# Stick-breaking attention in a hybrid block: the causal mask moved from a matrix product into the scan, and three copies of q moved from VectorE to ScalarE

## The chip, the core and the metric

The kernel runs on one core of a Trainium2 chip. The core has five engines with instruction queues of their own, each worked off in order: TensorE (PE, matrix products and transposes, into PSUM), VectorE (DVE), ScalarE (ACT, functions of one operand, copies and casts), GpSimd (POOL) and SyncE (SP, which here only issues DMAs). Engines wait for each other by semaphores. PE's weight loads have a row of their own in the profile, PEld. The metric is the time of one execution on the device in microseconds (us); several executions are timed, and one more is taken with the hardware profiler.

## The reference

One layer of a decoder trunk, for 1024 positions of width 1024 in float32. The part that matters is one of three head groups: attention of 8 heads of width 64 without a softmax. Keys take shares of a stick, the nearest first.

```python
def stick_breaking_attention(q, k, v):
    ...
        z = jnp.einsum('bqhd,bkhd->bhqk', qi, kj) * scale
        ...
        causal = s_pos < t_pos
        log_beta = jax.nn.log_sigmoid(z)
        log_rem = jnp.where(causal, jax.nn.log_sigmoid(-z), 0.0)
        suffix = lax.cumsum(log_rem, axis=3, reverse=True) - log_rem
        weights = jnp.where(causal, jnp.exp(log_beta + suffix), 0.0)
        o = jnp.einsum('bhqk,bkhd->bqhd', weights, vj)
```

q and k are RMS-normalised per head before that. A key that is not strictly before its query leaves the rest of the stick whole (factor 1) and gets weight 0.

## The kernel before

All matrix products are made of float32 halves: an operand is split into a high part, rounded to the type that PE multiplies (`split`: ScalarE makes the high part, VectorE or GpSimd the rest), and a product is three matmuls (`product`, L165 to L167), or two where one operand is used rounded.

The stages: the norm of the input and the gating group's projection; then for four pairs of heads the projection of q, k and v (`project`, PSUM tiles `qkv_ps`, two banks that it shares with the convolution's `cv_ps`) and the attention (`attend`); the convolution group; the output projection; the two large feed-forward products (`f_ps`, `d_ps`) and the gate (`g_ps`).

While the attention of pair n runs, the projection of pair n+1 (with the last pair, the convolution's projection) is woven between its pieces: `weave` draws from two generators in proportion to a count of matmuls. This order is the program's; a scheduler of the framework then sets each engine's order from a timeline of its own, so that a small change can move many instructions by some places.

`project` works on 8 tiles of 128 positions. Each tile fills a `qkv_ps` bank with 24 matmuls. ScalarE squares q and k (`qk_sq`), VectorE sums (`ss`), GpSimd takes the power (`rs`), VectorE scales (`qk`), and v is split into `V` (ScalarE, then VectorE, L141 and L142), which frees the bank. After every second tile `turn_qk` transposes q and k (`qk_tr`, in one of three PSUM banks that it shares with the attention's `w_tr`), and writes the high part of q (`QS`), its rest (`low_q`), the high part of k (`KH`) and its rest (`KL`, VectorE, which is the last reader of the `qk_tr` bank). The two heads of a pair lie in the lower and the upper 64 partitions. When a half of the positions is complete, joins build operands with 128 partitions: for k three copies on ScalarE (L411 to L413), for q three copies on VectorE (L414 to L416), each 64 x 512. There are 8 such sets, two for each pair.

`attend` has two pieces for each head and each pair of query blocks. `stick` computes for a query block t the product z over (t + 1) x 128 keys: one matmul with `KH` (L447), one with `KL` (L449), both with `QS` as weights, and for the 512 keys that hold the diagonal a third (L453), the identity times `below`, a constant tile that is -2^60 above the diagonal. ScalarE takes the Sigmoid of -z/8 (L454) into `rem`: the factor that a key leaves, 1 for a masked key. VectorE scans `rem` from the last key to the first, multiplying (L458), and the difference of neighbours (L464, on VectorE for t = 3, 5, 7 and otherwise on GpSimd) gives the weights `wt`. There are three buffers of `rem` and two PSUM banks for z. `gather` transposes the weights (`w_tr`, L486), splits them (`wT_hi`, `wT_lo`, L138 and L139) and multiplies them by `V` (`av`, L504).

Of the kernel before, what the change touches and what calls it, by code (L numbers as in the profile page):

```python
# [6 lines left out]

F32 = mybir.dt.float32
F32R = mybir.dt.float32r
AF = mybir.ActivationFunctionType  # L10
ALU = mybir.AluOpType
AX = mybir.AxisListType

P = 128
T = 1024
# [17 lines left out]
def hybrid_block(ctx: ExitStack, tc: tile.TileContext, a: dict):  # L33
# [5 lines left out]
    nc = tc.nc  # L39
    PSUM = bass.MemoryType.PSUM  # L40

    const = ctx.enter_context(tc.tile_pool(name="const", bufs=1))
# [61 lines left out]
    for _ in range(WARM):  # L104
        nc.tensor.matmul(warm[:, :P], ones, ones, start=True, stop=True)
    ident_r = const.tile([P, P], F32R, name="ident")
# [1 line left out]
    nc.gpsimd.memset(ident, 0.0)  # L108
    nc.gpsimd.affine_select(out=ident_r, in_=ident, pattern=[[-1, P]], base=0,
                            channel_multiplier=1, compare_op=ALU.not_equal, fill=1.0)  # L110

    below = const.tile([P, P], F32R, name="below")
    nc.gpsimd.memset(below.bitcast(F32), 0.0)
    nc.gpsimd.affine_select(out=below, in_=below.bitcast(F32), pattern=[[-1, P]], base=0,
                            channel_multiplier=1, compare_op=ALU.is_gt, fill=-2.0 ** 60)
    mhalf = const.tile([P, 8], F32, name="mhalf")
    nc.gpsimd.memset(mhalf, -0.5)

# [115 lines left out]
    attn_scope = ExitStack()  # L234
    at = attn_scope.enter_context(tc.tile_pool(name="at", bufs=2))
    lo_p, hi_p = slice(0, HD), slice(HD, P)

# [153 lines left out]
    def turn_qk(head, t, qk):  # L393

        QS, KH, KL, _, low_q = head
        th = t // 4
        tr = bank(ps_tr, "qk_tr")
        for i in range(2):
            for j in range(2):
                o = j * 256 + i * P  # L400
                nc.tensor.transpose(tr[:, o:o + P], qk[:, i, j * P:(j + 1) * P], ident)
        ws = slice((t % 4 - 1) * P, (t % 4 + 1) * P)

        split(tr[:, :256], QS[0][th][:, ws], low_q[th][:, ws], scale=gq)
        nc.scalar.activation(KH[0][th][:, ws], tr[:, 256:], AF.Copy, scale=gk)
        for hh, own in enumerate((lo_p, hi_p)):
            nc.vector.scalar_tensor_tensor(out=KL[hh][th][own, ws], in0=tr[own, 256:],
                                           scalar=gk[own], in1=KH[0][th][own, ws],
                                           op0=ALU.mult, op1=ALU.subtract)
        if t % 4 == 3:  # L410
            nc.scalar.copy(KH[1][th][hi_p], KH[0][th][hi_p])  # L411
            nc.scalar.copy(KH[1][th][lo_p], KH[0][th][hi_p])
            nc.scalar.copy(KH[0][th][hi_p], KH[0][th][lo_p])  # L413
            nc.vector.tensor_copy(QS[1][th][hi_p], QS[0][th][hi_p])  # L414
            nc.vector.tensor_copy(QS[1][th][lo_p], low_q[th][hi_p])
            nc.vector.tensor_copy(QS[0][th][hi_p], low_q[th][lo_p])  # L416
        return 8

    PROJECT = KT * 72 + 32
# [1 line left out]
    def attend(pr):  # L421
# [13 lines left out]
        def stick(hh, g):  # L435
            weights[hh, g] = []
            for t in (2 * g, 2 * g + 1):
                W = (t + 1) * P
                th, ts = block(t)

                rem = at.tile([P, T], F32, tag="rem", name=name("rem"), bufs=3)
                wt = at.tile([P, T], F32, tag="wt", name=name("wt"), bufs=4)
                for kh in reversed(range(th + 1)):
# [3 lines left out]
                    nc.tensor.matmul(z, QS[hh][th][:, ts], KH[hh][kh][:, :n],  # L447
                                     start=True, stop=False)
                    nc.tensor.matmul(z, QS[hh][th][:, ts], KL[hh][kh][:, :n],  # L449
                                     start=False, stop=kh < th)  # L450
                    if kh == th:

                        nc.tensor.matmul(z[:, n - P:], ident_r, below, start=False, stop=True)  # L453
                    last_act[0] = nc.scalar.activation(rem[:, ks], z, AF.Sigmoid,  # L454
                                                       scale=-HD ** -0.5)

                back = rem[:, :W][:, ::-1]
                nc.vector.tensor_tensor_scan(out=back, data0=back, data1=back, initial=1.0,  # L458
                                             op0=ALU.mult, op1=ALU.bypass)


                on_vector = t in (3, 5, 7)
# [882 lines left out]
```

## Time and profile before

| what | before |
|---|---|
| median of 3 runs | 1213.11 us (1210.53 to 1213.97) |
| the profiled execution's own time | 1212.77 us |
| its span, from its first to its last instruction | 1211.1 us |
| mean granted clock of TensorE | 0.995 |
| scans L458: number, busy time, median of one | 64, 90.6 us, 1.476 us |
| Sigmoids L454: number, busy time, mean of one | 96, 46.4 us, 0.500 us |

In the lists of groups a row gives the line in the kernel, the engine, the operation, the tile written and the tiles read (without buffer numbers), the partitions and elements, and how many there are; behind the bar come the busy time, the mean duration of one in ns, and the engine's idle time just before them with what ended it. A timeline row gives the start, the duration (of all that the row joins), and the same names. Durations of matmuls overlap, since they are pipelined.

### The profile page before, as it was taken

The page shows a single profiled execution, that of the slowest core. Times are in us where ns is not written, and L with a number is a line of the kernel's source. Part 1 is how long each engine was busy: PE and PEld are TensorE (multiplying, and loading weights), DVE is VectorE, ACT ScalarE, POOL GpSimd, SP SyncE. Part 2 cuts the span into 40 slices and gives each one's busy share as a digit, 9 for nine tenths or more (in the row PEclk, how much of TensorE's full clock was granted, in tenths as well). Part 3 has the DMA queues.
Part 4 walks back from the last instruction along what each step waited for, and adds up shares of the span by engine and source line. Part 5 has one row for each costly group of instructions (what it writes and reads, how often), then busy time and mean ns, then how long its engine had stood idle before and what let it go on. Part 6 is the DMA issues. An engine that isn't in the chain of part 4 may idle for free.

```text
span 1211.1 us, 17645 instructions
## 1 busy us (share of the span) xinstructions
PE 1188.3 (98%) x5852; PEld 1015.5 (84%) x5852; DVE 885.2 (73%) x1310; ACT 595.8 (49%) x1148; POOL 405.0 (33%) x472
## 2 busy tenths in 40 slices
PE   9999999999999999999999999999999999999997
PEld 7899899899878888888888888888888888888886
DVE  7846788989887667877877777787665656753597
ACT  7735555565643356734333343355443444546542
POOL 2324435465453312034453544421023301013412
PEclk9999999999999999999999999999999999999999
DMA  9602349989654776779998999677889975644857
GB/s 317 225 18 106 112 152 277 251 176 186 144 117 100 179 265 207 214 189 267 264 251 241 251 244 263 213 258 271 307 261 307 284 260 172 221 155 114 177 162 208
DMA packets 127964, 254.04 MB, mean 210 GB/s; under 512 B 14496, under 2 KB 22432, under 8 KB 127168
## 3 DMA queue, kind: packets, MB, share of 16 engines
q1 hardware_dynamic: 94992, 168.08, 41.5%
q0 software_dynamic: 27664, 57.05, 25.2%
q10 hardware_dynamic: 5216, 27.79, 6.3%
q8 instruction: 46, 0.75, 0.3%
q14 instruction: 46, 0.38, 0.1%
HBM read 192.30 MB, written 92.80 MB: 235 GB/s over the span
## 4 chain that ended last, share of the span: by engine, by line
PE 85%; DVE 7%; DMA 4%; issue 2%; ACT 1%; POOL 0%; ACTq 0%; SPq 0%; DVEq 0%; POOLq 0%
PE f_ps L814 25%; PE d_ps L814 25%; PE g_ps L814 6%; PE qkv_ps L165 3%; PE qkv_ps L166 3%; PE qkv_ps L167 3%; DVE rem L458 2%; PE av L504 2%; PE w_tr L486 2%; PE vu_ps L167 1%; PE vu_ps L165 1%; PE vu_ps L166 1%; PE o_ps L167 1%; PE o_ps L165 1%; PE o_ps L166 1%
## 5 line engine op out<-in xcount | busy, mean ns | idle before, releaser
L139 DVE TENSOR_TENSOR w_lo<-raw,w_hi 128x512 fp32r<-128x512 f32 x280 | 240.8, 864 | 87.4 <-ACT w_hi L138 85.5
L138 ACT CAST w_hi<-raw 128x512 fp32r<-128x512 f32 x280 | 172.0, 619 | 241.1 <-PE d_ps L814 121.0
L814 PE MATMUL f_ps<-hn_hi,w_hi 128*128 128x512 f32 x448 | 175.1, 392 | 0.0
L814 PE MATMUL f_ps<-hn_hi,w_lo 128*128 128x512 f32 x448 | 174.9, 391 | 0.0
L814 PE MATMUL f_ps<-hn_lo,w_hi 128*128 128x512 f32 x448 | 174.8, 390 | 0.0
L814 PE MATMUL d_ps<-f_hi,w_hi 128*128 128x512 f32 x448 | 174.8, 390 | 0.0
L814 PE MATMUL d_ps<-f_hi,w_lo 128*128 128x512 f32 x448 | 174.3, 389 | 0.0
L814 PE MATMUL d_ps<-f_lo,w_hi 128*128 128x512 f32 x448 | 174.3, 389 | 0.0
L458 DVE TENSOR_TENSOR_SCAN rem<-rem 128x128 f32<-128x128 f32 (+3 forms) x64 | 90.6, 1426 | 19.3 <-ACT rem L454 19.2
L814 PEld LDWEIGHTS f_ps<-hn_hi,w_hi 128*128 128x128 f32 x448 | 84.5, 189 | 17.8 <-issue 0.2
L814 PEld LDWEIGHTS f_ps<-hn_lo,w_hi 128*128 128x128 f32 x448 | 84.5, 189 | 17.7 <-issue 0.2
L814 PEld LDWEIGHTS f_ps<-hn_hi,w_lo 128*128 128x128 f32 x448 | 84.4, 188 | 17.8
L814 PEld LDWEIGHTS d_ps<-f_lo,w_hi 128*128 128x128 f32 x448 | 84.1, 188 | 17.8 <-issue 0.2
L814 PEld LDWEIGHTS d_ps<-f_hi,w_hi 128*128 128x128 f32 x448 | 84.1, 188 | 17.6 <-issue 0.2
L814 PEld LDWEIGHTS d_ps<-f_hi,w_lo 128*128 128x128 f32 x448 | 84.1, 188 | 17.5
L165 PE MATMUL qkv_ps<-whi,xn_hi 128*128 128x384 f32 x256 | 89.7, 350 | 1.1 <-DVE V L142 1.1
L167 PE MATMUL qkv_ps<-whi,xn_lo 128*128 128x384 f32 x256 | 87.6, 342 | 0.0
L166 PE MATMUL qkv_ps<-wlo,xn_hi 128*128 128x384 f32 x256 | 87.4, 341 | 0.0
L139 DVE TENSOR_TENSOR f_lo<-raw,f_hi 128x512 fp32r<-128x512 f32 x112 | 77.1, 718 | 9.6 <-ACT f_hi L138 9.3
L800 POOL TENSOR_TENSOR S<-S,sq 128x512 f32<-128x512 f32 x19 | 27.4, 1441 | 157.8 <-ACT sq L876 157.8
L138 ACT CAST f_hi<-raw 128x512 fp32r<-128x512 f32 x112 | 67.0, 620 | 23.3 <-DMA raw<-f_dram 20.0
L454 ACT ACTIVATE rem<-z 128x128 f32<-128x128 f32 (+3 forms) x96 | 46.4, 500 | 33.0 <-PE z L453 19.2
(252 smaller groups left out, 2656.2 us busy)
## 6 DMA issues: line engine op xcount, KB each, us to landing
raw<-in_w_ff SPq DMA_DIRECT2D x148, 256.0 KB, 4.0
raw<-f_dram SPq DMA_DIRECT2D x112, 256.0 KB, 4.9
raw<-w_sums SPq DMA_DIRECT2D x64, 256.0 KB, 4.1
f_dram<-f SPq DMA_DIRECT2D x48, 256.0 KB, 4.1
f_dram<-t SPq DMA_DIRECT2D x48, 256.0 KB, 3.8
w_sums<-in_w_ff POOLq DMA_DIRECT2D x8, 1024.0 KB, 12.5
w_sums<-w_sums POOLq DMA_DIRECT2D x8, 1024.0 KB, 13.1
raw<-in_w_out SPq DMA_DIRECT2D x28, 256.0 KB, 3.3
```

The source lines that it names most:

```text
L138: last_hi[0] = nc.scalar.copy(hi, src)
L139: low.tensor_tensor(out=lo, in0=src, in1=hi, op=ALU.subtract)
L165: nc.tensor.matmul(ps, lh, rh, start=first and i == 0, stop=False)
L166: nc.tensor.matmul(ps, lh, rl, start=False, stop=False)
L167: done = nc.tensor.matmul(ps, ll, rh, start=False, stop=last and i == len(terms) - 1)
L454: last_act[0] = nc.scalar.activation(rem[:, ks], z, AF.Sigmoid, scale=-HD ** -0.5)
L458: nc.vector.tensor_tensor_scan(out=back, data0=back, data1=back, initial=1.0, op0=ALU.mult, op1=ALU.bypass)
L486: nc.tensor.transpose(tr[:, n:n + P], wts[i][:, kb * P:(kb + 1) * P], ident)
L504: nc.tensor.matmul(av[:, first * P:], lhs, part[:, o:o + m], start=kb == 0 and part is hi, stop=kb == 2 * g + 1 and part is lo)
L800: return eng.tensor_tensor(out=out, in0=x, in1=y, op=ALU.add)
L814: done = nc.tensor.matmul(bank, l, r, start=first and k == 0 and i == 0, stop=k == len(b) - 1 and i == 2, skip_group_check=True)
```

## The change

The mask goes from the product into the scan. A tile `after` of bytes, 128 x 1024, is 0 except that its last 128 columns are 1 above the diagonal; it is built on GpSimd, behind the loads of the first constants. The scan reads it, aligned to the end of the keys and reversed as `rem` is, as its second operand, and its second operation becomes a maximum: at a masked key the running product is set to max(product, 1) = 1, elsewhere to max(product, 0), the product itself. `below` and the third matmul go, so that the `KL` matmul always ends the group. The three joins of q become copies on ScalarE.

```diff
-    below = const.tile([P, P], F32R, name="below")
-    nc.gpsimd.memset(below.bitcast(F32), 0.0)
-    nc.gpsimd.affine_select(out=below, in_=below.bitcast(F32), pattern=[[-1, P]], base=0,
-                            channel_multiplier=1, compare_op=ALU.is_gt, fill=-2.0 ** 60)
...
+    after = at.tile([P, T], INT8, name="after", bufs=1)
+    nc.gpsimd.memset(after, 0.0)
+    nc.gpsimd.affine_select(out=after[:, T - P:], in_=after[:, T - P:], pattern=[[-1, P]], base=0,
+                            channel_multiplier=1, compare_op=ALU.is_gt, fill=1.0)
...
-            nc.vector.tensor_copy(QS[1][th][hi_p], QS[0][th][hi_p])
-            nc.vector.tensor_copy(QS[1][th][lo_p], low_q[th][hi_p])
-            nc.vector.tensor_copy(QS[0][th][hi_p], low_q[th][lo_p])
+            nc.scalar.copy(QS[1][th][hi_p], QS[0][th][hi_p])
+            nc.scalar.copy(QS[1][th][lo_p], low_q[th][hi_p])
+            nc.scalar.copy(QS[0][th][hi_p], low_q[th][lo_p])
...
                     nc.tensor.matmul(z, QS[hh][th][:, ts], KL[hh][kh][:, :n],
-                                     start=False, stop=kh < th)
-                    if kh == th:
-
-                        nc.tensor.matmul(z[:, n - P:], ident_r, below, start=False, stop=True)
+                                     start=False, stop=True)
...
                 back = rem[:, :W][:, ::-1]
-                nc.vector.tensor_tensor_scan(out=back, data0=back, data1=back, initial=1.0,
-                                             op0=ALU.mult, op1=ALU.bypass)
+                nc.vector.tensor_tensor_scan(out=back, data0=back,
+                                             data1=after[:, T - W:][:, ::-1], initial=1.0,
+                                             op0=ALU.mult, op1=ALU.max)
```

The change moves instructions on every engine. Three places follow, each as the engine's order stands in the built program, before and then with the change (line numbers move by some lines; numbers in names are buffers).

PE, where the attention of the first pair begins: the products z of the first two query blocks. Before:

```order
L447 MATMUL z_1349<-KH_953,QS_954 128x128
L449 MATMUL z_1349<-KL_949,QS_954 128x128
L453 MATMUL z_1349<-below,ident 128x128
L447 MATMUL z_1423<-KH_953,QS_954 128x256
L449 MATMUL z_1423<-KL_949,QS_954 128x256
L453 MATMUL z_1423<-below,ident 128x128
L401 MATMUL qk_tr_1274<-ident,qk_1209 128x128 x2
```

With the change:

```order
L448 MATMUL z_1349<-KH_953,QS_954 128x128
L450 MATMUL z_1349<-KL_949,QS_954 128x128
L448 MATMUL z_1422<-KH_953,QS_954 128x256
L450 MATMUL z_1422<-KL_949,QS_954 128x256
L403 MATMUL qk_tr_1274<-ident,qk_1209 128x128 x2
```

The third product of each group is gone, and the transposes of the next tile follow two places earlier.

ScalarE at the first set of joins, in the projection of the first pair: `V` and `qk_sq` read the two `qkv_ps` banks. Before:

```order
L405 ACTIVATE KH_953<-qk_tr_1186,c_gk 128x256
L411 COPY KH_957<-KH_953 64x512
L412 COPY KH_957<-KH_953 64x512
L141 ACTIVATE V_1211<-qkv_ps_1161,r_731 128x2x64
L413 COPY KH_953<-KH_953 64x512
L374 ACTIVATE qk_sq_1239<-qkv_ps_1214 128x4x64
```

With the change:

```order
L407 ACTIVATE KH_953<-qk_tr_1186,c_gk 128x256
L413 COPY KH_957<-KH_953 64x512
L414 COPY KH_957<-KH_953 64x512
L416 COPY QS_956<-QS_954 64x512
L417 COPY QS_956<-q_lo_955 64x512
L137 ACTIVATE V_1211<-qkv_ps_1161,r_731 128x2x64
L415 COPY KH_953<-KH_953 64x512
L418 COPY QS_954<-q_lo_955 64x512
L376 ACTIVATE qk_sq_1239<-qkv_ps_1214 128x4x64
```

Two of q's joins stand ahead of `V`, and all three ahead of the next tile's square.

VectorE in the attention of the first pair, in the first long piece of PE's order that holds no product of a projection: from a 1024-wide scan to the two `KL`, which free the `qk_tr` bank, and the two `V`, which free the `qkv_ps` banks. Before:

```order
L458 SCALAR_TENSOR_TENSOR rem_1610<-rem_1610 128x1024
L139 TENSOR_TENSOR wT_lo_1659<-w_tr_1654,wT_hi_1658 128x384
L464 TENSOR_TENSOR wt_1611<-rem_1610 128x1023
L142 SCALAR_TENSOR_TENSOR q_lo_1411<-qk_tr_1680,c_gq,QS_1410 128x256
L382 TENSOR_TENSOR qk_1713<-qkv_ps_1718,rs_1793 128x256
L458 SCALAR_TENSOR_TENSOR rem_1692<-rem_1692 128x896
L458 SCALAR_TENSOR_TENSOR rem_1725<-rem_1725 128x1024
L407 SCALAR_TENSOR_TENSOR KL_1405<-qk_tr_1680,c_gk,KH_1409 64x256
L407 SCALAR_TENSOR_TENSOR KL_1407<-qk_tr_1680,c_gk,KH_1409 64x256
L142 SCALAR_TENSOR_TENSOR V_1715<-qkv_ps_1603,r_569,V_1715 128x2x64
L142 SCALAR_TENSOR_TENSOR V_1715<-qkv_ps_1718,r_569,V_1715 128x2x64
```

With the change, from the 896-wide scan on (the 1024-wide one, two `wT_lo` and a `wt` stand just ahead of it):

```order
L457 SCALAR_TENSOR_TENSOR rem_1684<-rem_1684,after 128x896
L135 TENSOR_TENSOR wT_lo_1651<-w_tr_1646,wT_hi_1650 128x384
L457 SCALAR_TENSOR_TENSOR rem_1716<-rem_1716,after 128x1024
L138 SCALAR_TENSOR_TENSOR q_lo_1410<-qk_tr_1672,c_gq,QS_1409 128x256
L457 SCALAR_TENSOR_TENSOR rem_1833<-rem_1833,after 128x640
L135 TENSOR_TENSOR wT_lo_1741<-w_tr_1735,wT_hi_1740 128x512
L464 TENSOR_TENSOR wt_1717<-rem_1716 128x1023
L135 TENSOR_TENSOR wT_lo_1756<-w_tr_1750,wT_hi_1755 128x512
L409 SCALAR_TENSOR_TENSOR KL_1404<-qk_tr_1672,c_gk,KH_1408 64x256
L409 SCALAR_TENSOR_TENSOR KL_1406<-qk_tr_1672,c_gk,KH_1408 64x256
L138 SCALAR_TENSOR_TENSOR V_1706<-qkv_ps_1596,r_569,V_1706 128x2x64
L138 SCALAR_TENSOR_TENSOR V_1706<-qkv_ps_1709,r_569,V_1706 128x2x64
```

(The scans print as SCALAR_TENSOR_TENSOR here.) A further scan, a `wt` and two `wT_lo` now stand ahead of `KL` and `V`. In PE's order the run of instructions between the two products of projections around this place holds 62 matmuls and transposes before and 83 with the change; the two next longest such runs hold 42 and 47 before, 55 and 57 now.

More of the change, by code (lines that the diff above doesn't have):

```diff
@@ L9 @@
 F32R = mybir.dt.float32r
+INT8 = mybir.dt.int8
 AF = mybir.ActivationFunctionType
```

## The prediction

> **What bounds the kernel now.** I read the page first, then the windows view, the waits view and the chain of waits inside the attention stage, and last the timeline at the places that the change touches.
>
> ```profile
> span 1211.1 us, 17645 instructions
> ...
> PE 1188.3 (98%) x5852; PEld 1015.5 (84%) x5852; DVE 885.2 (73%) x1310; ACT 595.8 (49%) x1148; POOL 405.0 (33%) x472
> ...
> PE 85%; DVE 7%; DMA 4%; issue 2%; ACT 1%; POOL 0%; ACTq 0%; SPq 0%; DVEq 0%; POOLq 0%
> ```
>
> TensorE (PE) is busy nearly all the span and is 85% of the chain that ended last. Everything that the change edits in the loop runs inside the attention stage, from 109 to 390 us by the mask product's row below. The windows view (a row: the stretch and its length, then the busy time of PE, PE's weight loads, VectorE, ScalarE, GpSimd, and PE's granted clock) says whether that stage is like the rest.
>
> ```profile
> 140.00:170.00 30.00, 25.67 (x159) 23.48 (x158) 28.26 (x38) 16.60 (x40) 13.53 (x13) 0.94 0.24 80
> 230.00:260.00 30.00, 29.05 (x198) 28.28 (x198) 28.88 (x48) 20.14 (x51) 18.23 (x28) 1.00 0.85 232
> 290.00:320.00 30.00, 30.00 (x201) 28.52 (x200) 28.76 (x53) 18.35 (x44) 13.74 (x20) 1.00 0.71 150
> 600.00:900.00 300.00, 300.00 (x1326) 248.39 (x1325) 220.40 (x273) 128.47 (x220) 99.62 (x92) 1.00 0.86 256
> ```
>
> From 600 to 900 us PE has no gap: what the attention stage saves is carried to the end and what it loses is not caught up. In the stage itself VectorE is as full as PE (28.9 of 30 us) and ScalarE has a third free (20.14 of 30 in the fullest row shown). So two engines set this stage, and the change takes work from both and gives some to the third. The waits of PE between 100 and 400 us, and the chain there by line:
>
> ```profile
> PE av L504 <- DVE wT_lo L139: 3.1, 4, 0.9
> PE w_tr L486 <- DVE KL L407: 2.8, 2, 2.0
> PE qk_tr L401 <- DVE qk L382: 1.3, 1, 1.3
> ...
> by line: PE qkv_ps L165 10.9%; PE qkv_ps L166 10.6%; PE qkv_ps L167 10.6%; DVE rem L458 9.4%; PE av L504 8.2%; PE w_tr L486 7.3%; issue 4.0%; PE cv_ps L165 3.5%; PE cv_ps L166 3.5%; PE cv_ps L167 3.5%; DVE wT_lo L139 3.4%; PE z L447 3.1%; P
> ```
>
> What PE waits for is VectorE. On the chain VectorE's scans and wT_lo alone hold 9.4 + 3.4 = 12.8% of 300 us, 38 us.
>
> **The mask product.** It goes 64 times (4 pairs, 2 heads, 8 query blocks). Matmuls overlap, so their own 0.22 us is not the price; the distance from one start to the next is.
>
> ```profile
> L453 PE MATMUL z<-below,ident x64: 218/223/309, 108.9 to 390.3; 128*128 128x128 f32 x64
> ...
> 202.59 0.28 PE L449 MATMUL z<-KL,QS 128*128 128x256 f32 x1
> 202.71 0.22 PE L453 MATMUL z<-below,ident 128*128 128x128 f32 x1
> 202.76 0.33 PE L504 MATMUL av<-wT_lo,V 128*128 128x256 f32 x1
> ...
> 388.38 0.28 PE L453 MATMUL z<-below,ident 128*128 128x128 f32 x1
> 388.49 0.45 PE L165 MATMUL cv_ps<-xn_hi,whi 128*128 128x512 f32 x1
> ```
>
> That is 0.05 us in the first place and 0.11 us in the second: 64 products are worth 3.2 to 7.0 us. I take the middle, 0.08 us: **-5.1**. Nothing stands in for them on PE. What is late next where a mask stood is the Sigmoid, which now follows the KL product.
>
> **The joins leave VectorE and come to ScalarE.** Each of the 8 sets has three; K's joins show ScalarE's price for the same shape (L415 reads as L414).
>
> ```profile
> L413 ACT CAST KH<-KH 64x512 fp32r<-64x512 f32 x8 | 5.0, 619 | 1.5 <-DVE KL L407 1.3
> L414 DVE CAST QS<-QS 64x512 fp32r<-64x512 f32 x8 | 3.4, 424 | 0.0
> L416 DVE CAST QS<-q_lo 64x512 fp32r<-64x512 f32 x8 | 3.4, 421 | 0.2
> ```
>
> VectorE loses 24 x 0.42 = 10.1 us, ScalarE gets 24 x 0.62 = 14.9. The gain lies between nothing (no engine is recorded as waiting for a join) and 10.1. I take a fifth, somewhat above VectorE's 12.8% of the chain since smaller VectorE groups are cut off that row: **-2.0**.
>
> On ScalarE the copies stand in order, so what is queued behind them is later. The first set:
>
> ```profile
> 102.53 0.62 ACT L412 CAST KH<-KH 64x512 fp32r<-64x512 f32 x1
> 103.18 0.37 ACT L141 ACTIVATE V<-qkv_ps,r 128x128 fp32r<-128x128 f32 x1
> ...
> 103.58 0.42 DVE L415 CAST QS<-q_lo 64x512 fp32r<-64x512 f32 x1
> 104.03 0.35 DVE L142 SCALAR_TENSOR_TENSOR V<-qkv_ps,r,V 128x128 fp32r<-128x128 f32 x1
> ...
> 104.53 0.41 PE L165 MATMUL qkv_ps<-whi,xn_hi 128*128 128x384 f32 x1
> ```
>
> Two joins now stand ahead of V there: ScalarE's V starts 1.24 us later, at 104.42, VectorE's V (free by then, its joins are gone) follows at about 104.8 and frees the PSUM bank at 105.2. PE wants a bank at 104.53: 0.7 us lost. The third join and the moved K join put the next square sum 1.9 us back, but its bank is wanted only one projection tile later. The other seven sets lie among attention work, which PE can do meanwhile. At worst each costs 1.24, 9.9 in all; at best nothing. I take the first set alone: **+0.8**.
>
> **The moved order.** With the masks gone, more attention work stands between one projection tile and the next in PE's order: the three longest runs of PE instructions without a projection product grow from 62, 42 and 47 to 83, 55 and 57. In such a run PE waits for VectorE. The first one before:
>
> ```profile
> 138.60 0.34 PE L167 MATMUL qkv_ps<-whi,xn_lo 128*128 128x384 f32 x1
> ...
> 152.73 0.66 PE L486 MATMUL w_tr<-ident,wt 128*128 128x128 f32 x4 [1.98 <-DVE KL L407]
> 153.14 0.42 PE L165 MATMUL qkv_ps<-whi,xn_hi 128*128 128x384 f32 x1
> ...
> 141.69 1.28 DVE L139 TENSOR_TENSOR wT_lo<-w_tr,wT_hi 128x512 fp32r<-128x512 f32 x2
> 142.88 2.48 DVE L458 TENSOR_TENSOR_SCAN rem<-rem 128x1024 f32<-128x1024 f32 x1
> ...
> 145.73 1.21 DVE L464 TENSOR_TENSOR wt<-rem 128x1023 f32<-128x1023 f32 x1
> ...
> 147.59 4.19 DVE L458 TENSOR_TENSOR_SCAN rem<-rem 128x896 f32<-128x896 f32 x2
> 151.70 0.97 DVE L407 SCALAR_TENSOR_TENSOR KL<-qk_tr,c_gk,KH 64x256 fp32r<-64x256 f32 x2
> ```
>
> The bank that KL frees ends PE's wait. Before, VectorE needs 141.69 to 151.70, 10.0 us, from the two wT_lo to KL. In the new order there stand in that piece also a 640-wide scan, one more wt of 1.21 and two more wT_lo (0.64 each), while a reduction and a q tile (0.8 together) stand ahead of it. The 640-wide scan lies between the 512- and the 768-wide ones below, about 1.5. So KL comes 1.5 + 1.2 + 1.3 - 0.8 = 3.2 us later or a little more, and behind KL stand two dozen PE rows, 24 x 0.11 = 2.7 us (a 256-wide one takes 0.12 above), before the projection goes on. That moves it 5.9 us later, with 25 more rows of useful work in the run, some 3.2 us at 0.13: 2.7 lost. In the second run one more scan, 896 wide (4.19 / 2 = 2.1 us), is pulled ahead of KL, and 13 more rows (16 come, 3 masks go), 16 x 0.1, cover all but 0.6; in the third VectorE's order is the same up to one small tile. I take 2.7 + 0.6 = **+3.3**, between -1 (the work pulled ahead covers all and relieves VectorE later) and +7.
>
> The timeline has a second price at that place:
>
> ```profile
> 153.75 0.33 PE L165 MATMUL qkv_ps<-whi,xn_hi 128*128 128x384 f32 x1
> 153.92 0.38 PE L166 MATMUL qkv_ps<-wlo,xn_hi 128*128 128x384 f32 x1
> ...
> 154.41 0.52 PE L165 MATMUL qkv_ps<-whi,xn_hi 128*128 128x384 f32 x1
> 154.73 0.52 PE L166 MATMUL qkv_ps<-wlo,xn_hi 128*128 128x384 f32 x1
> ```
>
> Behind the wait the spacing goes from 0.17 to 0.32 us (clock 0.94 in that 30 us window, so 1.8 us are lost). The run before pays this once; the sum keeps it at once. The Trainium skill (TensorE: Matmul & The Clock Gate, "What's actually happening") says that the array drops to half clock after about 3.4 us of too little work; by that rule, which speaks against this change, longer runs pay it more often, and the sum would be 1.8 us higher for each further time. The trace agrees with the halving; no row here shows the threshold.
>
> **The scan.** Its second operand becomes a tile of bytes and its second operation a maximum; no row shows either.
>
> ```profile
> L458 DVE TENSOR_TENSOR_SCAN rem<-rem 128x768 f32<-128x768 f32 x8 | 14.4, 1799 | 4.3 <-ACT rem L454 4.3
> L458 DVE TENSOR_TENSOR_SCAN rem<-rem 128x512 f32<-128x512 f32 x8 | 10.1, 1264 | 0.2 <-ACT rem L454 0.2
> L464 DVE TENSOR_TENSOR wt<-rem 128x511 f32<-128x511 f32 x8 | 5.9, 738 | 0.1
> ```
>
> A subtraction of two f32 tiles of 511 takes 0.74 us, the scan 1.26, so the scan is not set by its reads, and narrower reads win nothing. If the maximum cost one more such pass, all scans (36,864 columns) would take 72 x 0.74 = 53 us more. I take **0**, since the old scan already reads two operands and makes two operations per column. The mask tile is built on GpSimd behind the constants' loads, long before the first scan: 0.
>
> **Sum.** -5.1 - 2.0 + 0.8 + 3.3 = -3.0 on the profiled execution's own 1212.8, which stands 0.3 under the median of 1213.1: **1209.8**, -0.25 to -0.27%.
>
> **Rivals.**
> 1. VectorE's relief counts in full: joins -10.1, masks -5.1, the first set +0.8, runs +2: -12.4, 1200.4. For it: VectorE ends nearly all of PE's waits, and z reaches the Sigmoid earlier. Against: VectorE is not the later engine all through the stage (290 to 320: PE 30.00). What lies halfway, 1203 to 1208, belongs here too.
> 2. The change does not do what it says: the masks ran in the shadow of VectorE's waits, the joins were in no one's way. Then only the masks outside the long runs count, about 52 x 0.08 = 4.2, and the runs (+3.3) and the first set (+0.8) take it back: -0.1, 1212.7.
> 3. The runs without projection decide, slower: 7 in place of 3.3 and two more half-clock stretches of 1.8: -5.1 - 2.0 + 0.8 + 7 + 3.6 = +4.3, 1217.1. It decides from 6.3 us of added waits in the three runs (zero gain) and is measurable from 9.9. For it: VectorE is full there. Against: the same VectorE work is then missing later.
> 4. The scan is dearer. VectorE has 1.1 to 1.7 us of 30 free in the rows above, some 13 over 281 us and perhaps 20 with the stage's ends; 53 - 10 us would pass that by 23, less 3.0: 1233. Against: above.
>
> **How the numbers follow.** I call differences under 0.3% (3.6 us) no change, about what a measurement of this kernel can tell. Forecast 0.48 (own range 1206 to 1213: 0.16 faster, 0.32 same); rival 1, 0.27 (faster); rival 2, 0.11 (same); rival 3, 0.10 (slower); rival 4, 0.04 (slower). Faster 0.43, same 0.43, slower 0.14. The range 1200 to 1217 leaves out rival 4, half of rival 3 and the lower edge of rival 1, some 0.15.
>
> **What would show it.** Masks: no such group, and the KL product followed by the next row at 0.05 us or its own length. Joins: 24 at 0.62 us on ScalarE, VectorE's busy time down by 10. Scans: 1.26 us at 512 and 1.80 at 768 as before; 2.0 at 512 is rival 4. Runs: the first from 138.8 to about 159 in place of 153.1, and half clock more than once for rival 3. First set: a 0.7 us wait of qkv_ps for V near 105 us. It would be wrong if the end of the stage (last z at 390) moved by more than 10 us either way, or if what it gained were lost again before 450.

## The result and the profile after

| | before | with the change |
|---|---|---|
| median | 1213.22 us of 4 runs (1210.53 to 1213.97) | 1221.32 us of 4 runs (1220.52 to 1223.28) |
| ratio to before, 95% interval | 1 | 1.0069 (1.0049 to 1.0089) |
| profiled execution, its span | 1212.77, 1211.1 | 1221.38, 1219.7 |
| last z product ends the stage near | 390.3 us | 401.3 us |
| first row of the output projection (`o_ps`) | 416.2 us | 426.5 us |

The change makes the kernel slower by 8.1 us, where 3 us less were forecast. The page after: span, busy times, and the chain that ended last.

```profile
span 1219.7 us, 17543 instructions
...
PE 1186.2 (97%) x5788; PEld 1011.6 (83%) x5788; DVE 878.2 (72%) x1286; ACT 608.4 (50%) x1172; POOL 409.1 (34%) x472
...
PE 83%; DVE 7%; ACT 3%; DMA 3%; issue 2%; POOL 1%; SPq 0%; ACTq 0%; DVEq 0%; POOLq 0%
```

64 matmuls and 24 VectorE copies are gone, PE has 2.1 us less to do, and the span is 8.6 us longer. VectorE's busy time fell by 7.0 us, ScalarE's rose by 12.6, and ScalarE's share of the chain rose from 1 to 3%. The windows view after, for the stretches shown of before (start and end, length, busy time of PE, PEld, VectorE, ScalarE, GpSimd, then PE's granted clock):

```profile
140.00:170.00 30.00, 23.11 (x120) 20.11 (x120) 29.07 (x29) 13.94 (x31) 9.61 (x10) 0.83 0.48 175
230.00:260.00 30.00, 28.34 (x195) 27.74 (x194) 25.43 (x40) 18.26 (x46) 14.64 (x21) 1.00 0.86 231
290.00:320.00 30.00, 26.13 (x171) 24.60 (x172) 26.45 (x37) 17.10 (x40) 16.71 (x17) 1.00 0.83 149
600.00:900.00 300.00, 300.00 (x1326) 248.39 (x1325) 227.72 (x272) 127.14 (x219) 102.70 (x92) 1.00 0.87 259
```

From 600 to 900 us PE is full, as before: the loss is made in the attention stage and most of it, 8.6 of 11.0 us, is carried to the end (1.6 of the rest come back where the trace of before has a stretch of half clock at 522.7 us that this one has not). In the stage PE got 120 matmuls done from 140 to 170 us in place of 159, at a clock of 0.83 in place of 0.94, while VectorE was as full as before; from 290 to 320 us PE, full before, is 26.13 busy. PE's waits between 100 and 410 us (what waits, for what: us in total, times, longest):

```profile
PE av L504 <- DVE wT_lo L135: 5.4, 3, 3.3
PE qkv_ps L161 <- DVE V L138: 3.8, 4, 1.6
PE w_tr L486 <- DVE wt L464: 2.8, 3, 1.3
PE w_tr L486 <- DVE KL L409: 2.4, 2, 1.2
PE av L504 <- ACT y_both L513: 2.4, 2, 1.7
PE z L448 <- ACT QS L418: 1.9, 1, 1.9
```

Three kinds stand out against before. The waits for V were one of 1.1 us and are now four of 3.8 together. The wait of z for a join (QS, L418) and those of `av` for ScalarE's copy of the last `av` (`y_both`) are new in this list: 4.3 us. The second of these is not the joins' alone, as experiment 3 shows. The rows of the scan and of a join in the list of groups:

```profile
L457 DVE TENSOR_TENSOR_SCAN rem<-rem,after 128x768 f32<-128x768 f32 x8 | 15.0, 1880 | 4.6 <-ACT rem L452 4.6
L457 DVE TENSOR_TENSOR_SCAN rem<-rem,after 128x512 f32<-128x512 f32 x8 | 10.9, 1368 | 1.0 <-ACT rem L452 1.0
L418 ACT CAST QS<-q_lo 64x512 fp32r<-64x512 f32 x8 | 4.9, 615 | 0.0
```

A scan takes some 0.1 us more in the mean (1.37 at 512 in place of 1.26, 1.88 at 768 in place of 1.80), which a few long ones make: the median at 512 is 1.22 in place of 1.21. Nothing like another pass shows, which would be 2.0 at 512. Joins take 0.62 us on ScalarE, as priced.

**Where the joins stop PE.** The timeline of ScalarE, VectorE and PE at the first set:

```profile
103.98 0.62 ACT L414 CAST KH<-KH 64x512 fp32r<-64x512 f32 x1
...
104.63 0.62 ACT L416 CAST QS<-QS 64x512 fp32r<-64x512 f32 x1
...
105.27 0.62 ACT L417 CAST QS<-q_lo 64x512 fp32r<-64x512 f32 x1
...
105.92 0.37 ACT L137 ACTIVATE V<-qkv_ps,r 128x128 fp32r<-128x128 f32 x1
...
106.32 0.35 DVE L138 SCALAR_TENSOR_TENSOR V<-qkv_ps,r,V 128x128 fp32r<-128x128 f32 x1 [1.66 <-ACT V L137]
106.78 0.19 PEld L161 LDWEIGHTS qkv_ps<-whi,xn_hi 128*128 128x128 f32 x1 [0.83 <-PE qkv_ps L163]
```

Two joins stand ahead of V, V is late, and PE's weight loads stop for 0.83 us. So far it is what the prediction worked out. The same at the second set, a hundred us later (ScalarE, then PE):

```profile
202.16 0.62 ACT L414 CAST KH<-KH 64x512 fp32r<-64x512 f32 x1
202.81 0.62 ACT L416 CAST QS<-QS 64x512 fp32r<-64x512 f32 x1
203.45 0.62 ACT L417 CAST QS<-q_lo 64x512 fp32r<-64x512 f32 x1
203.97 0.57 ACT L134 CAST wT_hi<-w_tr 128x512 fp32r<-128x512 f32 x1
204.57 0.62 ACT L415 CAST KH<-KH 64x512 fp32r<-64x512 f32 x1
205.09 0.61 ACT L418 CAST QS<-q_lo 64x512 fp32r<-64x512 f32 x1
```

```profile
203.51 0.34 PE L163 MATMUL qkv_ps<-whi,xn_lo 128*128 128x384 f32 x1
205.76 0.33 PE L448 MATMUL z<-KH,QS 128*128 128x128 f32 x1 [1.91 <-ACT QS L418]
```

The next row of PE's order is a z that reads the new half of q, and the last join is the sixth copy of its set on ScalarE, with one `wT_hi` among them. PE has attention work of its own further down its queue, but its queue is in order: it waits 1.91 us.

**The half clock.** The windows of the first long stretch without a projection product, which ends at 164.4 us, cut where the granted clock changes:

```profile
140.00:149.20 9.20, 5.74 (x29) 3.81 (x28) 8.33 (x6) 6.09 (x13) 4.38 (x4) 1.00 0.62 230
149.20:156.00 6.80, 5.93 (x24) 5.54 (x25) 6.80 (x7) 1.83 (x4) 2.19 (x2) 0.50 0.00 0
156.00:159.40 3.40, 1.43 (x9) 0.94 (x8) 3.40 (x4) 1.99 (x7) 0.54 (x2) 1.00 0.30 96
159.40:162.80 3.40, 2.81 (x11) 2.74 (x12) 3.34 (x6) 1.32 (x4) 0.00 (x0) 0.50 1.35 501
```

Two stretches of half clock, 10.2 us in all, where the kernel before had one of 3.4 us at 154.1; a third of 3.4 us begins at 207.2, behind the wait of z just shown. In these 22.8 us PE is busy 15.9 (the sum of the second figures), and VectorE is full from 149.2 on. What PE waits for in this stretch is not KL, as the prediction had it, but above all a `wT_lo` that stands behind a 1024-wide scan of 3.46 us, and then `y_both`:

```profile
150.06 0.58 PE L504 MATMUL av<-wT_lo,V 128*128 128x256 f32 x1 [3.27 <-DVE wT_lo L135]
158.78 0.39 PE L504 MATMUL av<-wT_hi,V 128*128 128x256 f32 x1 [1.74 <-ACT y_both L513]
```

### The profile page after: what moved, and what is told of

It reads as the page before. It is cut to its first block, busy times and chain, and to the rows that moved or that the text cites. A ratio compares the mean times of both kernels' runs of the same rounds, so it can differ in the third digit from the quotient of the medians.

```text
span 1219.7 us, 17543 instructions
## 1 busy us (share of the span) xinstructions
PE 1186.2 (97%) x5788; PEld 1011.6 (83%) x5788; DVE 878.2 (72%) x1286; ACT 608.4 (50%) x1172; POOL 409.1 (34%) x472
## 4 chain that ended last, share of the span: by engine, by line
PE 83%; DVE 7%; ACT 3%; DMA 3%; issue 2%; POOL 1%; SPq 0%; ACTq 0%; DVEq 0%; POOLq 0%
PE f_ps L814 25%; PE d_ps L814 25%; PE g_ps L814 6%; DVE rem L457 3%; PE qkv_ps L161 2%; PE qkv_ps L162 2%; PE qkv_ps L163 2%; PE av L504 2%; PE o_ps L163 2%; PE o_ps L161 2%; PE o_ps L162 2%; PE cv_ps L163 2%; PE cv_ps L162 2%; PE cv_ps L161 2%; PE w_tr L486 1%
## 5 line engine op out<-in xcount | busy, mean ns | idle before, releaser
L135 DVE TENSOR_TENSOR w_lo<-raw,w_hi 128x512 fp32r<-128x512 f32 x280 | 248.9, 893 | 90.5 <-ACT w_hi L134 88.5
L457 DVE TENSOR_TENSOR_SCAN rem<-rem,after 128x128 f32<-128x128 f32 (+3 forms) x64 | 93.4, 1467 | 14.0 <-ACT rem L452 12.1
L170 POOL TENSOR_TENSOR rs<-ss,mhalf 128x4 f32<-128x4 f32 x32 | 43.9, 1373 | 65.4 <-DVE ss L379 65.3
```

The lines of the kernel that those rows point to most:

```text
L135: low.tensor_tensor(out=lo, in0=src, in1=hi, op=ALU.subtract)
L170: last_power[0] = nc.gpsimd.tensor_tensor(out=out, in0=in_, in1=mhalf[:, :n], op=ALU.pow)
L457: nc.vector.tensor_tensor_scan(out=back, data0=back, data1=after[:, T - W:][:, ::-1], initial=1.0, op0=ALU.mult, op1=ALU.max)
```

## The experiments

Every row below compares with runs of the kernel before on the same chip, made beside its own. Each run also lists PE's mean granted clock, so (1 - clock) x span, which is half of the time spent at half clock, is what half clock may have cost at most; the mean over a kernel's runs is in the column "half-clock loss", and "rest" is the median over the runs of each run's time less its own loss. In the profiles 3.4 to 4.2 us of that loss lie behind the last product. "Order" is the order of PE's matmuls in the attention stage: the kernel's own, as the scheduler's timeline draws it, or that of another kernel.

| kernel | masks | q's joins on | order | ratio (95%) | median us | half-clock loss | rest |
|---|---|---|---|---|---|---|---|
| before, beside these runs | product | VectorE | own | 1 | 1212.9 to 1213.7 | 5.7 to 6.4 | 1207.0 to 1207.4 |
| the change | scan | ScalarE | own | 1.0069 (1.0049 to 1.0089) | 1221.3 | 10.1 | 1211.6 |
| scan_only | both | VectorE | own, that of before | 0.9998 (0.9989 to 1.0007) | 1212.9 | 5.3 | 1207.2 |
| mask_only | scan | VectorE | own | 0.9992 (0.9981 to 1.0003) | 1211.5 | 5.8 | 1205.4 |
| joins_only | product | ScalarE | own | 1.0020 (1.0009 to 1.0030) | 1214.6 | 5.8 | 1209.5 |
| order_short | scan | ScalarE | own, a weave number altered | 1.0141 (1.0124 to 1.0157) | 1228.7 | 13.8 | 1216.5 |
| after_short | scan | ScalarE | of mask_only | 1.0057 (1.0044 to 1.0070) | 1220.8 | 6.3 | 1214.6 |
| mask_long | scan | VectorE | of the change | 1.0020 (1.0008 to 1.0033) | 1215.4 | 8.5 | 1207.3 |
| seven_long | scan | VectorE first set, ScalarE seven | of the change | 1.0058 (1.0037 to 1.0079) | 1221.1 | 10.2 | 1211.4 |
| before_long | product | VectorE | of the change | 1.0124 (1.0108 to 1.0140) | 1228.2 | 10.7 | 1217.8 |
| mask_old | scan | VectorE | of before | 1.0029 (1.0013 to 1.0045) | 1216.9 | 12.8 | 1204.1 |
| joins_old | product | ScalarE | of before | 1.0043 (1.0030 to 1.0057) | 1219.1 | 6.7 | 1211.8 |
| after_old | scan | ScalarE | of before | 1.0060 (1.0037 to 1.0083) | 1220.0 | 10.2 | 1210.7 |
| pool_old | scan | GpSimd | of before | 1.0025 (1.0015 to 1.0036) | 1216.4 | 9.8 | 1206.7 |
| twice_old | scan | VectorE, K's joins twice on ScalarE | of before | 1.0040 (1.0019 to 1.0060) | 1219.4 | 9.6 | 1209.1 |
| mask_attend | scan | VectorE | own, weave count 788 | 0.9935 (0.9913 to 0.9958) | 1206.4 | 6.8 | 1199.4 |
| after_attend | scan | ScalarE | own, weave count 788 | 1.0111 (1.0085 to 1.0136) | 1227.1 | 13.5 | 1214.5 |
| before_attend | product | VectorE | own, weave count 788 | 1.0000 (0.9988 to 1.0011) | 1213.6 | 8.4 | 1205.0 |

The first theory was **order**: the loss comes from the longer stretches of PE rows without a projection product. Its rivals were **joins** (ScalarE's copies hold PE up) and **scan** (its new form is dear).

**1. One part at a time.** mask_only is the change with q's joins left on VectorE, joins_only the kernel before with them on ScalarE, and scan_only the kernel before with the scan of the change.

```diff
 joins_only, against before
-            nc.vector.tensor_copy(QS[1][th][hi_p], QS[0][th][hi_p])
+            nc.scalar.copy(QS[1][th][hi_p], QS[0][th][hi_p])
 (and so the two others)
```

> Masks moved into the scan as in the change, q's joins left on VectorE. The three longest stretches of PE rows without a projection product are 55, 43 and 45 here (62, 42 and 47 before; 83, 55 and 57 with the change). Theory order (the change loses because those stretches became longer): 1206 to 1212 us, since the masks are gone and the stretches are not longer. Theory joins (ScalarE's copies stand ahead of V and of the squares and PE waits for them): 1206 to 1210 us, as here they are away. Theory scan (byte operand and maximum cost VectorE's time): 1218 us or more, as both are here.

> q's joins go to ScalarE as in the change, the mask product and the old scan are kept. Longest stretches without a projection product: 65, 47 and 42. Theory order: within 3 us of before, 1211 to 1216, as the stretches are those of before within a few rows. Theory joins: the change's loss is here, 1219 to 1226 (the change's +8 and the 5 us that the masks would have saved). Theory scan: at or below before, 1209 to 1213.

> The scan takes the byte tile and the maximum as in the change, but the mask product is kept too (masked twice, same result) and the joins stay on VectorE; PE's order is that of before, row for row in its long stretches (62, 42, 47). Theory order and theory joins: 1213 us within 2. Theory scan: 1217 us or more.

The scan costs nothing: 0.9998, and its durations in the trace are those of before (1.264 us in the mean at 512 in both). The masks alone gain 1 us, not 5, within an interval that reaches from 2.3 us of gain to a loss of 0.4; the joins alone lose 2.4, and together they lose 8.1: the parts don't add up, and each of the three kernels has an order of its own.

**2. The same instructions, another order.** One number of the weave, by which a query block's products are counted.

```diff
-                yield 2 * (t + 1) + 10
+                yield 2 * (t + 1) + 14
```

> The change in full, with one number of the weave altered (a query block's products counted as 2(t+1)+14 in place of +10 units of work), so the same instructions stand in another order: longest stretches without a projection product 62, 41 and 32 in place of 83, 55 and 57. Theory order: the loss is gone, 1206 to 1214 us. Theory joins: nothing about the joins is altered, so it stays at 1218 to 1222. Theory scan: stays at 1218 to 1222.

A miss for both theories: the long stretches were shorter and the time 7.4 us longer. The number also shifts which projection work stands beside which attention (the last z stood at 416.4 us in place of 401.3), so it was no clean test. The next ones hold PE's order itself fixed.

**3. PE's order tied.** Behind the program, an edge of issue order ties each of the 1,623 matmuls from the first z to the last to the one that precedes it in another kernel's order. No edge makes an engine wait for another; the scheduler orders the other engines around it.

```diff
+        chain(nc, tc)
...
+    for one, two in zip(ROWS, ROWS[1:]):
+        tc.add_manual_dep(made[two], made[one].name, mybir.DependencyInfo(
+            mybir.DependencyClass.NoSync, mybir.DependencyReason.DATA), reason="order")
```

> The changed kernel, instruction for instruction, but PE's 1,623 matmuls of the attention stage are tied to the order that they have with q's joins on VectorE (long stretches without a projection product 55, 43 and 45 in place of 83, 55 and 57). Theory order (the loss comes from PE's order, which the timeline of the scheduler drew, not from what the joins or the scan cost): 1212 to 1215 us, that is 1211.6 of the masks alone and 0.5 to 3 for the joins. Theory joins (ScalarE's copies hold up V, squares and the q of a new half, and without masks nothing fills that): 1219 to 1222, as with the change.

> The converse: q's joins on VectorE, masks in the scan, but PE's matmuls of the attention stage tied to the order of the changed kernel (83, 55 and 57). Theory order: 1217 to 1221 us with no join on ScalarE. Theory joins: 1210 to 1213, as in the run with the masks alone.

> The changed kernel with PE's matmuls of the attention stage in the order that they have in the kernel before, the masks left out (57, 39 and 43). Theory order: 1209 to 1214 us; if the masks are worth the 5 us that I gave them, 1208 to 1211. Theory joins: 1218 to 1222.

> The kernel before, masks, joins and scan as they were, but with the PE order of the changed kernel (90, 60 and 62 with the masks in it). Theory order: 1219 to 1225 us, as all that costs is here and nothing that saves. Theory joins: 1212 to 1215.

The theory of the order falls as the main cause. With the joins on ScalarE the time is 1.0057 to 1.0069 in these three orders, long stretches or short (order_short's own order, at 1.0141, shows that another order can still cost more). With them on VectorE the order of the change costs 1.0020 - 0.9992 = 0.0028, 3.4 us. At one and the same order, the joins cost 0.0065 (after_short less mask_only, 7.9 us) and 0.0049 (the change less mask_long, 5.9 us). With the intervals of both rows combined, these three differences are known to about 2, 2 and 3 us (an estimate). before_long, whose mask products are not tied, gives 15 us for the order in a kernel with masks; why so much more than the 3.4 was not tried. Turned round, mask_long less before_long makes the masks worth 0.0104, 12.6 us, in the order of the change.

Since mask_long and the change have one PE order, their rows can be laid side by side: the change falls behind at V (0.8 us near 106, 0.7 near 246, 0.9 near 275), at z's wait for the join (1.05 near 206) and at `av`'s wait for `y_both` (0.87 near 314). It loses 1.6 us more in the rows at half clock behind 207, and gains 1.1 near 157, where both wait for `y_both`, mask_long 2.88 us and the change 1.74. So the wait for `y_both` near 157 belongs to the order, and the one near 314 to the joins. At that last place the change has, on ScalarE and then on PE:

```profile
312.00 0.62 ACT L416 CAST QS<-QS 64x512 fp32r<-64x512 f32 x1
312.64 0.62 ACT L417 CAST QS<-q_lo 64x512 fp32r<-64x512 f32 x1
313.27 0.37 ACT L137 ACTIVATE V<-qkv_ps,r 128x128 fp32r<-128x128 f32 x1
313.54 0.36 ACT L513 COPY y_both<-av 128x256 f32<-128x256 f32 x1
```

```profile
313.95 0.38 PE L504 MATMUL av<-wT_hi,V 128*128 128x256 f32 x1 [0.63 <-ACT y_both L513]
```

and mask_long, with the same PE rows, no join there and no wait:

```profile
305.94 0.62 ACT L414 CAST KH<-KH 64x512 fp32r<-64x512 f32 x1
306.59 0.37 ACT L137 ACTIVATE V<-qkv_ps,r 128x128 fp32r<-128x128 f32 x1
306.85 0.36 ACT L513 COPY y_both<-av 128x256 f32<-128x256 f32 x1
```

**4. The two parts in the order of before.** joins_old and mask_old do one part each; pool_old does the change with the joins on GpSimd; twice_old leaves q's joins on VectorE and makes K's three joins twice on ScalarE, with the same values.

```diff
 pool_old, against the change
-            nc.scalar.copy(QS[1][th][hi_p], QS[0][th][hi_p])
+            nc.gpsimd.tensor_copy(QS[1][th][hi_p], QS[0][th][hi_p])
 (and so the two others)
 twice_old, ahead of q's joins on VectorE
             nc.scalar.copy(KH[1][th][hi_p], KH[0][th][hi_p])
             nc.scalar.copy(KH[1][th][lo_p], KH[0][th][hi_p])
+            nc.scalar.copy(KH[1][th][hi_p], KH[0][th][hi_p])
+            nc.scalar.copy(KH[1][th][lo_p], KH[0][th][hi_p])
             nc.scalar.copy(KH[0][th][hi_p], KH[0][th][lo_p])
+            nc.scalar.copy(KH[0][th][hi_p], KH[0][th][lo_p])
```

> Masks in the scan, q's joins on VectorE, PE's matmuls of the attention stage tied to the order of the kernel before (masks left out): what the mask products alone are worth. My sum gave them 5 us (3.2 to 7.0): 1206 to 1210 us. If the masks ran in the shadow of VectorE's waits: 1211 to 1213.

> The kernel before with q's joins on ScalarE and PE's order of before, masks kept: what the joins alone are worth in one and the same order. Theory queue (the copies stand on ScalarE ahead of V and of av's copy, and each of the eight sets stops PE for a part of a us): 1217 to 1222 us, as much above before as the change with that order is above the masks alone with it. Theory order (the joins matter only by the order that the scheduler draws): 1211 to 1214.

> The changed kernel with q's three joins on GpSimd, in place of ScalarE, PE's order of before: VectorE is relieved of 24 copies and ScalarE gets none. Theory queue: the loss is gone unless GpSimd's copies are themselves late for z, 1206 to 1212 us; against the masks alone in the same order it shows what VectorE's relief is worth (I gave 2 us of 10). If the loss came from anything but ScalarE's queue: 1218 or more.

> Masks in the scan, q's joins on VectorE, PE's order of before, and K's three joins each made twice on ScalarE, with the same values: ScalarE has as many copies as in the change, but its order puts the second ones behind V and behind av's copy. Theory queue (it is the place ahead of V and of av's copy that costs): within 3 us of the run with the masks alone in this order. If ScalarE's added work costs wherever it stands: 6 us or more above that run.

The joins cost 5.2 us with the masks kept (joins_old, 3.6 to 6.9), as the theory of ScalarE's queue expected. Row by row against before, in the same order of PE, joins_old falls behind at V (0.83 us near 104.5), at a `wT_lo` (1.39 near 173), at z's wait for a join (0.56 near 264) and at the wait for `y_both` (0.63 near 300). Without the masks the joins cost 0.0031 or 3.8 us (after_old less mask_old), known to some 3 us either way. On GpSimd (0.61 to 0.72 us each) the time is that of mask_old and 4 us under after_old: the loss is gone. What VectorE's relief brings can't be read from this pair, since pool_old has waits of its own in the trace (2.15 us of z for GpSimd's last join, 2.76 for V near 113) and lacks a stop of 3.8 us that mask_old has. twice_old stays within 3 us of mask_old, but not because the place behind V is free of charge: the 0.83 us at the first set are gone, and z now waits for K's last copy, 1.77 us near 202.5 and 1.62 near 270.7. As these traces read, the price is that of six copies on the way from `qk_tr` to z, and where V or `av`'s copy stands behind them, theirs as well; in time, twice_old and mask_old are not apart beyond the intervals.

The miss is mask_old: without the mask products, in the order of before up to a few early rows, the time is 3.5 us longer. The windows view of scan_only, which has this order with the masks kept, at two of its fullest places of VectorE:

```profile
150.00:160.00 10.00, 7.71 (x36) 7.20 (x37) 9.94 (x12) 2.75 (x7) 3.51 (x1) 0.83 0.57 210
218.00:228.00 10.00, 9.79 (x64) 9.21 (x65) 9.95 (x13) 5.15 (x13) 3.74 (x6) 1.00 1.12 212
```

and of mask_old:

```profile
150.00:160.00 10.00, 6.98 (x25) 5.94 (x25) 9.94 (x11) 4.01 (x11) 3.51 (x1) 0.71 0.43 151
218.00:228.00 10.00, 7.08 (x35) 6.29 (x34) 9.95 (x13) 4.66 (x12) 4.70 (x5) 0.83 1.12 209
```

The same rows stand 1 to 2 us later in mask_old in the first window and up to 5 in the second. VectorE (third busy time) is full in both kernels, so PE cannot be earlier; it only waits more, and the granted clock falls from 0.83 to 0.71 and from 1.00 to 0.83. Over all runs the half-clock loss is 12.8 us in place of 5.3, and the rest is 3.1 us shorter. But between these places PE catches up, and at 284 us mask_old stands only 1.8 us behind. The larger part of the loss in this trace has another cause, a stop of ScalarE for a DMA that holds two Sigmoids and so z for 3.8 us (ScalarE, then PE):

```profile
289.55 0.37 ACT L513 COPY y_both<-av 128x256 f32<-128x256 f32 x1 [3.98 <-DMA y_dram<-y_both]
289.82 1.09 ACT L452 ACTIVATE rem<-z 128x512 f32<-128x512 f32 x2
```

```profile
290.48 0.33 PE L448 MATMUL z<-KH,QS 128*128 128x128 f32 x1 [3.80 <-ACT rem L452]
```

With the half clock behind it, mask_old stands 6.1 us behind at 288 us of scan_only's time and 4.2 at the end of the stage. The traces of pool_old, twice_old and after_old, which have this order and no masks too, show no such stop. Whether the other runs of mask_old have it isn't known, so how much of the 3.5 us comes from the missing mask products stays open.

**5. One set or eight; and an order that suits.** seven_long puts the first set of joins back on VectorE. The others count an attention pair as 788 units of work in the weave, in place of 808, which breaks up the second and the third long stretch.

```diff
 seven_long
+            q_copy = nc.vector.tensor_copy if head is heads[0] and th == 0 else nc.scalar.copy
-            nc.scalar.copy(QS[1][th][hi_p], QS[0][th][hi_p])
+            q_copy(QS[1][th][hi_p], QS[0][th][hi_p])
 (and so the two others)
 mask_attend, after_attend, before_attend
-    ATTEND = 2 * (72 + 8 * 10 + 72 + 10 * 10 + 80)
+    ATTEND = 2 * (72 + 8 * 10 + 72 + 10 * 10 + 80) - 20
```

> The changed kernel with its PE order of the attention stage tied, and the first set of q's joins back on VectorE: the other seven sets stay on ScalarE. In this order all eight sets on VectorE took 1215.4 us and all eight on ScalarE 1221.3. If each set stops PE by itself: 1219.5 to 1221. If only the first set costs anything, as I predicted: 1214.5 to 1216.5.

> Masks in the scan, q's joins on VectorE, and the weave counts an attention pair at 788 in place of 808 units, which breaks up the second and the third long stretch without a projection product (55, 22 and 27 the longest, in place of 55, 43 and 45). If the second and third stretch cost what the traces show in them (3.9 and 4.7 us of waiting) and nothing takes their place: 1204 to 1208 us, faster than before. If the waiting only moves to other places: 1210 to 1213.

> The change in full with the weave's count at 788: the long stretches are 83, 26 and 24 in place of 83, 57 and 55. If the order of the second and third stretch holds the change's loss: 1211 to 1215 us. If it is the joins on ScalarE and the first stretch: 1218 to 1222.

> The kernel before with the weave's count at 788 (longest stretches without a projection product 62, 28 and 22 in place of 62, 47 and 42), mask product, old scan and joins as they were. Against the run with the masks in the scan and the same count (1206.4 us) it tells what the mask products are worth in an order that suits both. If the order alone made that run faster: 1205 to 1208 us. If the masks are worth what my sum gave them: 1209 to 1213.

Seven sets cost 1.0058 - 1.0020 = 0.0038, 4.6 us, and all eight 5.9, each known to some 3 us: enough to tell the seven from nothing, not the seven from the eight. Near 204 us PE waits in seven_long as it did in the change:

```profile
204.04 0.33 PE L449 MATMUL z<-KH,QS 128*128 128x128 f32 x1 [2.36 <-ACT QS L419]
```

mask_attend is faster than both kernels: 1206.4 us, 0.65% under before (0.42 to 0.87). The masks' move is needed for it, since before_attend gains nothing from the same number: between the two lie 7.2 us, each in the order that the scheduler drew for it. PE's waits in the stage of mask_attend are those below; two that the change has, for a join and for `y_both`, are not among them.

```profile
PE av L504 <- ACT wT_hi L134: 3.3, 1, 3.3
PE qkv_ps L161 <- DVE V L138: 2.5, 3, 1.2
PE av L504 <- DVE wT_lo L135: 2.2, 2, 1.8
PE w_tr L486 <- DVE wt L464: 1.8, 2, 1.6
```

after_attend, with the joins on ScalarE and only one long stretch left, is slower than the change, as the theory of the joins expected in sign but not in size: besides its waits for V (five, 6.0 us together) the convolution's VectorE work comes so late that the output projection waits for it:

```profile
431.86 0.76 PE L161 MATMUL o_ps<-y_hi,wo_hi 128*128 128x512 f32 x1 [5.28 <-DVE cv_acc L663]
```

Why that work is late there was not tried. One more run, mask_ahead, breaks up the same two stretches by another number, a head start of the attention of 40 in place of 26 units (55, 24 and 23). It was expected at 1204 to 1208 us and took 1212.8, 0.9993 (0.9974 to 1.0012); its output is wrong (relative error 0.077), so that time is only a hint. With it, order_short, after_attend and before_attend have shorter second and third stretches and gain nothing, so their length alone is not what makes mask_attend fast, and why 788 suits it is not shown.

## Why the prediction was wrong

Point by point, against its sum of -5.1 - 2.0 + 0.8 + 3.3:

- **Joins on ScalarE, +0.8: the step that failed.** "The other seven sets lie among attention work, which PE can do meanwhile." In the trace the first set stops PE for the 0.8 us that were taken, and the other seven cost 4.6 us (seven_long against mask_long). PE's queue is in order, and its next row is often the very z, `av` or projection tile that waits for ScalarE. The upper end given for this term was 9.9; all eight came to 5.9 net of VectorE's relief, and the value taken was next to the lower end. The price per set was worked out from V alone; the wait of z for the last join (1.91 us near 206) and that of `av` for `y_both` were not in it.
- **Joins off VectorE, -2.0: not seen.** VectorE's busy time fell by 7.0 us, not 10, since the scans grew by 2.8 in all. In pool_old, where nothing goes to ScalarE, the time is that of mask_old within 0.5 us, but GpSimd's own lateness and mask_old's stop are in that figure, so the relief alone stays open; with the first point, the two terms on the joins were -1.2 together and measured +5.9.
- **Masks, -5.1: the second step that failed; the masks' worth is not a constant.** -12.6 us in the order of the change, -7.2 between before_attend and mask_attend (5.6 of it in the rest), -1.0 in the scheduler's own order, +3.5 in the order of before (there the rest is 3.1 to 3.3 shorter, and the trace holds the DMA stop). The step took a distance between row starts as time saved. Where VectorE ends PE's waits, the same distance becomes wait, and half clock.
- **Moved order, +3.3: right in size, by a pair of runs, and in part by luck.** mask_long less mask_only is 3.4 us. The reason given for the longer stretches, "With the masks gone", is wrong: with the masks alone gone they are 55, 43 and 45, with the joins alone moved 65, 47 and 42, and only the two together draw 83, 55 and 57. The place was misread too: the first stretch ended at 164.4 us, where about 159 had been worked out, and what PE waited for in it was `wT_lo` (3.27 us) and `y_both` (1.74), not KL; half clock is part of it.
- **Half clock kept at one stretch: wrong.** There are three in the stage. The rule of the Trainium skill that was weighed in the prediction (TensorE: Matmul & The Clock Gate, "What's actually happening": half clock after at least one idle window of some 3.4 us) spoke for more of them; the trace agrees in that each stretch lasts 3.4 or 6.8 us, and differs in that PE was not idle all through the 3.4 us ahead of one: it was busy 1.42 of them ahead of 154.1 us before, and 1.49 ahead of 207.2 us with the change. The half-clock loss is 10.1 us in the change's runs and about 6 in those of before: some 4 of the 8.1 us at most. It stands in and behind the waits above, and mask_long, in the same order of PE and without ScalarE's new joins, has 8.5; that it has no cause of its own is argued from this and not shown.
- **Scan, 0: right** (scan_only).

Put together at one order: before to mask_long +2.4 us (masks and order, -1.8 in the sum), and mask_long to the change +5.9 (joins, -1.2 in the sum). So of the some 11 us between forecast and result about 7 lie in the joins and 4 in the masks. Rival 3, the stretches and half clock, came nearest with 1217.1; mask_long, which has its stretches, took 1215.4, and what it lacked are the joins. The forecast's test for "wrong", a stage that ends more than 10 us later, came in: the last z moved by 11.0 us.

## What to carry to other kernels

A copy that moves to an engine with a third of its time free is priced by what stands behind it in that engine's queue, at every place where it stands: free time in a 30 us window says nothing of the two us between a transpose and the matmul that wants its result. Removing work from an engine that waits saves nothing at the waits, and where a scheduler redraws the order around a change, the change should be measured in one fixed order and then with the order's numbers tuned anew: the same masks in the scan were worth from -13 to +3.5 us in four orders. Here the part worth keeping is the mask in the scan, with q's joins left on VectorE and the weave's count lowered.

## What the runs showed of the hardware that was not expected

- With 64 matmuls of 0.22 us taken out of PE, rows otherwise in nearly the same order, the half-clock loss rose from 5.3 to 12.8 us (mean of 11 and 9 runs, scan_only and mask_old). In the profile of mask_old half clock stood in or right behind four waits of PE of 1.9 to 3.8 us (near 122, 155, 222 and 290 us), three that VectorE ends and one that the DMA stop makes; with the masks kept there was one such stretch.
- Half clock came without an idle stretch of 3.4 us: in the 3.4 us ahead of its start PE was busy 1.31 us (mask_old, 123.4 us), 1.42 (before, 154.1) and 1.49 (the change, 207.2).
- A maximum with a tile of bytes as the scan's second operand costs no more than the old bypass: 1.264 us in the mean at 128 x 512 in both, and within 0.1% in the kernel's time (scan_only).
- A cast of 64 x 512 took 0.42 us on VectorE, 0.62 on ScalarE and 0.61 to 0.72 on GpSimd.
